# A decoder block in fp32 on one core: the opening's row tiles turned one by one, two channels to a bank, with fewer warming matmuls

## The chip, the core and the metric

One core of one Trainium2 chip runs the whole program. The metric is the device time of one execution in microseconds; lower is better. The kernel before took 797.24 us, the median of three runs (797.21 to 797.54). The profiles quoted below are of one further execution, in which the profiler ran along.

## The reference

Input is x, 512 positions of 1024 channels in fp32, and the parameters of one layer:

```
h = rmsnorm(x, norm1_g);  z = h @ w_in + b_in          # 1024 -> 6656 columns
z_glu, z_rx, z_rg, z_ga, z_gb = split(z)
u   = silu(layernorm(causal_conv31(z_glu[:1024] * sigmoid(z_glu[1024:]))))
y_a = u @ conv_w_out + conv_b_out
xb  = causal_conv4(z_rx);  hb = rg_lru(xb)              # gates from two block-diagonal products, a scan
y_b = (hb * gelu(z_rg)) @ lru_w_out
x   = x + (sigmoid(z_ga) * y_a + sigmoid(z_gb) * y_b) @ w_mix_out
h   = rmsnorm(x, norm2_g)
x   = x + (silu(h @ ffn_w1) * (h @ ffn_w3)) @ ffn_w2
out = rmsnorm(x, norm_f_g)
```

The change lies in the first line: the first normalization, the turn of its result so that channels lie on partitions, and the first two column blocks of the product with w_in.

## The kernel before, in words

**Precision and weights.** Every operand of a large product is split into a high part and a low part in the type fp32r, and a product is three matmuls: high weight by high input, high weight by low input, low weight by high input (`mm3`, line 525). Weights come in chunks of 128 columns (`w_in_chunk`, line 191; raw tile, high part, low part in `emit_chunk`, line 150, and `split_to`, line 121): SyncE issues the load of 512 KB, ScalarE casts the high part (line 123), GpSimd subtracts for the low part (line 119). `emit_to(n)` (line 180) emits chunks up to the n-th. In the opening the first two chunks' high parts are cast by VectorE, and the second one's low part also comes from VectorE: the class `Later` (line 145) only keeps the operands of that subtraction, and `norm1_rows` issues it at a place of its own (line 652).

**The opening.** x is loaded as four row tiles of 128 positions, each as two halves of 512 channels (`load_x`, line 488). For each row tile, `norm1_rows` (line 591) has ScalarE square and sum both halves (lines 550 and 556), VectorE and ScalarE make the inverse root (lines 551, 557, 558), and VectorE scale both halves in place (line 595). `turn_half` (line 567) then turns two row tiles: for each of the eight channel blocks c, TensorE turns a 128 x 128 block of either tile into a PSUM bank of its own (line 574), ScalarE writes the high part h1{c}h with norm1_g as scale (line 582) and VectorE the low part h1{c}l (line 583). norm1_g itself is loaded as a row block and turned by `rows_turned` (line 513; turn in line 517, copy to `par` in line 518); the other parameter rows follow in two more calls. "First half" below means row tiles 0 and 1 (positions 0 to 255), "second half" row tiles 2 and 3.

**The first products.** `early_mm(i, hf)` (line 602) multiplies column block 0 (i = 0) or 8 (i = 1) of w_in with one half of the positions, 256 columns wide, so that products can start when half of the input is turned; its matmuls stand under line 534. For the first half, the eight low-weight products stand last. All later products are 512 wide.

**Banks.** PSUM has eight banks of 128 x 512: six in the pool `bank`, two in `bank2`, given out in turn. A tile waits for the readers of the tile that had its bank before.

**Warming.** 21 matmuls of 128 x 128 on a tile of ones (line 506) stand ahead of everything on TensorE.

**Order.** The opening (lines 640 to 665) is under `manual_schedule`: TensorE, ScalarE, VectorE and SyncE keep the order in which the code stands there. GpSimd's order, and everything after, is set by the framework's scheduler. Waits are put in by the framework: an instruction waits for a count of the engine that it depends on, and dependences through PSUM are kept by the bank.

**After the opening** the kernel takes the other 50 column blocks of w_in, 24 matmuls each, with the convolutions, the gates and the scan beside them, then the products with lru_w_out, conv_w_out and w_mix_out, the feed-forward products (partly by a scheme with seven products instead of eight), and the last normalization. TensorE is given a product of some kind all the way.

Of the kernel before, what the change touches and what calls it, by code (L numbers as in the profile page):

```python
# [33 lines left out]
RAW = 4  # L34
HL = 5
AHEAD = 4
WARM = 21

FEW, MANY = 32, 112

# [46 lines left out]
def tile_block(ctx, tc, a, out):  # L87
# [19 lines left out]
    def bank(name):  # L107
        return psum.tile([P, T], F32, tag="mm", name=name)
# [404 lines left out]
    def rows_turned(c0, c1):  # L513
        pt = bank2(f"par_ps{c0}")
        for c in range(c0, c1, P):
            m = min(P, c1 - c)
            pe.transpose(pt[:, c - c0 : c - c0 + m], rowt[row_at(c)[0]][:m, :P], ident[:m, :m])
        vec.tensor_copy(par[:, c0:c1], pt[:, : c1 - c0])
        return pt

    def pc(name, i):
        return par[:, col[name] + i : col[name] + i + 1]


    def mm3(ps, ws, xs, lo_last=False):


        n = 3 * len(ws)
        i = 0
        three = [((wh, xh), (wh, xl), (wl, xh)) for (wh, wl), (xh, xl) in zip(ws, xs)]  # L530
        if lo_last:
            three = [q[:2] for q in three] + [q[2:] for q in three]
        for l, r in (q for qs in three for q in qs):
            pe.matmul(ps, l, r, start=i == 0, stop=i == n - 1)  # L534
            i += 1

    def w_tiles(key, kt, ahead=AHEAD):
        h, l = weights(key, ahead)
        return [(h[:, k, :], l[:, k, :]) for k in range(kt)]
# [21 lines left out]
    def rstd_of(halves, junk, between=None):  # L561
        begun = rstd_begin(halves[0], junk[0])
        if between:
            between()
        return rstd_end(begun, halves[1], junk[1])

    def turn_half(name, rows, gname, dest, hf, bk, some=range(ND), full=None):

        cs = slice(hf * 256, hf * 256 + 256)
        for c in some:  # L570
            ps = bk[c % len(bk)](f"{name}{hf}{c}")
            for t in range(2):
                src = rows[2 * hf + t][c // 4][:, (c % 4) * P : (c % 4 + 1) * P]
                pe.transpose(ps[:, t * P : (t + 1) * P], src, ident)  # L574
            g = pc(gname, c)
            h, l = (v[:, cs] for v in dest[c])
            if full:
                f = full[c][:, cs]
                newest["half"] = act.activation(f, ps[:, :256], AF.Copy, scale=g).ins
                _, _, last = split_to(h, l, f, vec)  # L580
                continue
            act.activation(h, ps[:, :256], AF.Copy, scale=g)
            last = vec.scalar_tensor_tensor(out=l, in0=ps[:, :256], scalar=g, in1=h.bitcast(F32), op0=ALU.mult, op1=ALU.subtract)
        return last.ins

    def parts_of(pair_tiles, cs=slice(0, T)):
        return [(h[:, cs], l[:, cs]) for h, l in pair_tiles]

    h1p = [pairt(f"h1{c}") for c in range(ND)]

    def norm1_rows(t, between=None):
        junk = [shortt(f"n1j{t}{h}") for h in range(2)]
        r = rstd_of(xt[t], junk, between)
        for h in range(2):
            vec.tensor_scalar(out=xt[t][h], in0=xt[t][h], scalar1=r, scalar2=None, op0=ALU.mult)

    HALVES = [slice(0, 256), slice(256, 512)]
    EARLY = 1
    EARLY_IN = [(GLU + j + 8 * o) for j in range(EARLY) for o in range(2)]
    early = []  # L600

    def early_mm(i, hf):
        m = EARLY_IN[i]
        if hf == 0:
            early.append((m, w_tiles(f"in{m}", ND, 0), bank(f"z{m}")))
        _, ws, ps = early[i]
        mm3(ps[:, HALVES[hf]], ws, parts_of(h1p, HALVES[hf]), lo_last=hf == 0)


    c4, c8 = (consts.tile([P, NR], F32, name=n) for n in ("c4", "c8"))  # L610
# [27 lines left out]

    ET = mybir.EngineType
    with tc.manual_schedule(engines={ET.PE, ET.Activation, ET.DVE, ET.SP}):  # L640
        norm1_rows(0)
        norm1_rows(1)
        rows_turned(0, ROWS[0][1])
        emit_to(1, vec.tensor_copy)
        turn_half("tx", xt, "norm1_g", h1p, 0, [bank, bank, bank, bank2])
        later = Later()
        emit_to(2, vec.tensor_copy, later)
        load_x(2)
        load_x(3)
        for i in first[1:]:  # L650
            load_rows(i)
        norm1_rows(2, lambda: vec.tensor_tensor(**later.operands))
        norm1_rows(3)
        for i in range(len(parts)):
            if i not in first:
                load_rows(i)
        early_mm(0, 0)
        early_mm(1, 0)
        turn_half("tx", xt, "norm1_g", h1p, 1, [bank2, bank, bank])
        emit_to(3)  # L660
        early_mm(0, 1)
        lru_factors(rows_turned(ROWS[0][1], n_first)[:, 2 * P :])
        emit_to(4)
        early_mm(1, 1)
        rows_turned(n_first, n_rows)
    h1 = parts_of(h1p)

# [623 lines left out]
```

## Time and profile before

| | |
|---|---|
| median of three runs | 797.24 us (797.21 to 797.54) |
| the profiled execution | 797.7 us |
| its span, first to last instruction | 795.9 us |
| first matmul on TensorE | 1.09 us |
| first product of w_in (line 534) | 10.70 us |
| first 512-wide product | 25.52 us |

Rows of the timeline have start and duration in us, engine, line, operation, what is written and read, the count of merged instructions, and in brackets the idle time before them with what ended it. PE is TensorE's matmuls, PEld its weight loads, DVE is VectorE, ACT ScalarE, POOL GpSimd, SPq the issue of DMAs by SyncE. Buffer numbers are left out, so `z<-h10h,hl_in` stands for each product with h10h. A turn shows as a matmul `tx<-ident,x`.

### The profile page before, as it was taken

The page shows a single profiled execution, that of the slowest core. Times are in us where ns is not written, and L with a number is a line of the kernel's source. Part 1 is how long each engine was busy: PE and PEld are TensorE (multiplying, and loading weights), DVE is VectorE, ACT ScalarE, POOL GpSimd, SP SyncE. Part 2 cuts the span into 40 slices and gives each one's busy share as a digit, 9 for nine tenths or more (in the row PEclk, how much of TensorE's full clock was granted, in tenths as well). Part 3 has the DMA queues.
Part 4 walks back from the last instruction along what each step waited for, and adds up shares of the span by engine and source line. Part 5 has one row for each costly group of instructions (what it writes and reads, how often), then busy time and mean ns, then how long its engine had stood idle before and what let it go on. Part 6 is the DMA issues. An engine that isn't in the chain of part 4 may idle for free.

```text
span 795.9 us, 12177 instructions
## 1 busy us (share of the span) xinstructions
PE 789.2 (99%) x4369; PEld 690.5 (87%) x4369; DVE 673.2 (85%) x1020; ACT 471.7 (59%) x683; POOL 228.8 (29%) x181
## 2 busy tenths in 40 slices
PE   9999999999999999999999999999999999999997
PEld 8888888888888888888888898999999999888885
DVE  6699899999989988786787889978878887889757
ACT  6646585987768855563335575545455555577443
POOL 1855766797666856030000000000000000000000
PEclk9999999999999999999999999999999999999999
DMA  6945646487555664368847545566555553676652
GB/s 213 257 130 143 187 144 208 121 247 208 173 168 173 213 182 120 128 203 263 276 160 243 172 134 158 131 171 181 155 133 133 133 133 106 210 258 207 198 173 106
DMA packets 184604, 140.29 MB, mean 176 GB/s; under 512 B 14259, under 2 KB 162143, under 8 KB 184543
## 3 DMA queue, kind: packets, MB, share of 16 engines
q1 hardware_dynamic: 183103, 134.27, 55.2%
q0 software_dynamic: 1440, 5.24, 3.5%
q8 instruction: 34, 0.56, 0.3%
q14 instruction: 27, 0.22, 0.1%
HBM read 113.79 MB, written 18.64 MB: 166 GB/s over the span
## 4 chain that ended last, share of the span: by engine, by line
PE 99%; DVE 0%; issue 0%; ACT 0%
PE z L534 36%; PE or L953 13%; PE ft L1080 7%; PE yb L534 7%; PE fa L1080 7%; PE fr L1080 6%; PE ya L534 5%; PE mxr L953 5%; PE fe L1080 4%; PE g L827 3%; PE fb L1080 2%; PE f L534 2%; PE warm L506 1%; PE f L1106 1%; PE tx L574 1%; PE th L574 0%
## 5 line engine op out<-in xcount | busy, mean ns | idle before, releaser
L702 DVE SCALAR_TENSOR_TENSOR cv<-u,par,cv 128x511 f32<-128x511 f32 (+19 forms) x240 | 162.4, 730 | 5.0 <-ACT cv L699 4.7
L119 POOL TENSOR_TENSOR hl_in<-raw_in,hl_in 128x1024 fp32r<-128x1024 f32 x51 | 123.5, 2426 | 83.1 <-ACT hl_in L123 69.6
L355 POOL DMA_DIRECT2D raw_fb<-raw_fb x10 | 8.7, 874 | 298.4 <-DVE raw_fb L357 186.1
L119 POOL TENSOR_TENSOR ows<-ows 128x256 f32<-128x256 f32 x66 | 56.7, 861 | 37.7 <-DMA ows<-in_ffn_w_dram 34.7
L123 ACT CAST hl_ft<-raw_fb 128x1024 fp32r<-128x1024 f32 x40 | 41.8, 1048 | 32.5 <-DVE raw_fb L357 17.0
L123 ACT CAST hl_in<-raw_in 128x1024 fp32r<-128x1024 f32 x50 | 52.1, 1043 | 10.4 <-PE z L534 6.6
L119 DVE TENSOR_TENSOR hl_ft<-raw_fb,hl_ft 128x1024 fp32r<-128x1024 f32 x40 | 48.5, 1220 | 7.0 <-ACT hl_ft L123 6.9
L119 DVE TENSOR_TENSOR hl_fb<-raw_fb,hl_fb 128x1024 fp32r<-128x1024 f32 x30 | 36.6, 1221 | 9.5 <-ACT hl_fb L123 9.3
L357 DVE TENSOR_TENSOR raw_fb<-raw_fb,raw_fb 128x1024 f32<-128x1024 f32 x20 | 24.5, 1225 | 20.3 <-DMA raw_fb<-in_ffn_w_dram 20.0
L534 PE MATMUL z<-h10h,hl_in 128*128 128x512 f32 (+1 forms) x108 | 41.5, 385 | 0.0
L534 PE MATMUL z<-h17h,hl_in 128*128 128x512 f32 (+1 forms) x108 | 41.1, 381 | 0.0
L534 PE MATMUL z<-h13h,hl_in 128*128 128x512 f32 (+1 forms) x108 | 41.1, 381 | 0.0
L534 PE MATMUL z<-h15h,hl_in 128*128 128x512 f32 (+1 forms) x108 | 41.1, 381 | 0.0
L534 PE MATMUL z<-h14h,hl_in 128*128 128x512 f32 (+1 forms) x108 | 41.1, 381 | 0.0
L534 PE MATMUL z<-h16h,hl_in 128*128 128x512 f32 (+1 forms) x108 | 41.1, 381 | 0.0
L534 PE MATMUL z<-h12h,hl_in 128*128 128x512 f32 (+1 forms) x108 | 41.1, 381 | 0.0
L534 PE MATMUL z<-h11h,hl_in 128*128 128x512 f32 (+1 forms) x108 | 41.1, 381 | 0.0
L123 ACT CAST hl_fb<-raw_fb 128x1024 fp32r<-128x1024 f32 x30 | 31.4, 1047 | 8.9 <-PE mxr L953 3.7
L119 DVE TENSOR_TENSOR hl_ob<-raw_ob,hl_ob 128x1024 fp32r<-128x1024 f32 (+1 forms) x23 | 27.0, 1174 | 11.0 <-ACT hl_ob L123 10.9
L123 ACT CAST hl_ob<-raw_ob 128x1024 fp32r<-128x1024 f32 (+1 forms) x23 | 23.3, 1015 | 21.6 <-PE or L953 10.8
L1080 PE MATMUL fe<-hs_0h,hl_ft 128*128 128x256 f32 x160 | 30.7, 283 | 0.0
L1080 PE MATMUL ft<-hs_1h,hl_ft 128*128 128x256 f32 x160 | 30.4, 283 | 0.0
(1016 smaller groups left out, 2610.0 us busy)
## 6 DMA issues: line engine op xcount, KB each, us to landing
raw_in<-in_w_in_dram SPq DMA_DIRECT2D x52, 512.0 KB
raw_fb<-in_ffn_w_dram SPq DMA_DIRECT2D x96, 256.0 KB
ows<-in_ffn_w_dram SPq DMA_DIRECT2D x44, 256.0 KB
os<-ows SPq DMA_DIRECT2D x22, 512.0 KB
raw_ob<-in_ffn_w_dram SPq DMA_DIRECT2D x33, 256.0 KB
raw_ot<-os SPq DMA_DIRECT2D x33, 256.0 KB
raw_lo<-in_lru_w_out_dram SPq DMA_DIRECT2D x16, 320.0 KB
raw_fb<-raw_fb POOLq DMA_DIRECT2D x10, 512.0 KB, 4.6
```

Source lines behind the costliest of these rows:

```text
L119: return eng.tensor_tensor(out=o, in0=x, in1=y, op=ALU.subtract)
L123: copy(h, full)
L355: pool_e.dma_start(out=q, in_=y, accum_op=ALU.add)
L357: vec.tensor_tensor(out=q, in0=q, in1=y, op=ALU.add)
L506: pe.matmul(wp[:, :P], ones, ones, start=True, stop=True)
L534: pe.matmul(ps, l, r, start=i == 0, stop=i == n - 1)
L574: pe.transpose(ps[:, t * P : (t + 1) * P], src, ident)
L702: vec.scalar_tensor_tensor(out=acc[c][:, s:], in0=u[c][:, : T - s], scalar=dw(c, s), in1=acc[c][:, s:], op0=ALU.mult, op1=ALU.add)
L827: pe.matmul(ps, l, r, start=k == 0, stop=k == len(mms) - 1)
L953: pe.matmul(banks[i], l_[:, ts], r_, start=start and n == 0, stop=stop and n == 2, skip_group_check=again)
L1080: pe.matmul(ps[:, HALVES[i]], lw[:, 4 * i + c, :], rx_, start=not (again or i or c or m), stop=bool(i and c == 3 and m == 2), skip_group_c ...
L1106: pe.matmul(plain_1[:, cs], l, r, start=k == 0 and m == 0, stop=k == ND - 1 and m == 2)
```

## The change

- The opening has 12 warming matmuls instead of 21.
- `turn_half` isn't used in the opening any more (it stays for the second normalization). `turn_rows` turns one row tile, all eight channel blocks, as soon as that tile is scaled; `split_rows` then makes the high and low parts of a half. Four banks take the eight channel blocks of a half: blocks c and c + 4 share a bank.
- The turn of norm1_g stands between the turns of row tiles 0 and 1 instead of ahead of both.
- In column block 0's product with the first half, three of the eight low-weight products (of channel blocks 0, 1 and 2) stand among the products that wait for the input: after block 5's, after block 6's, and again after block 6's.
- Row tiles 2 and 3 are normalized by `norm1_pair`: row tile 3's first sum of squares and its small VectorE instruction stand before the scaling of row tile 2.
- In the second half, the turns take two banks of `bank2` and two of `bank`.
- Some calls change places without a change in any engine's own order (`emit_to(3)` and `emit_to(4)` against `early_mm`).

```
-WARM = 21
+WARM = 12
...
-    def norm1_rows(t, between=None):
-        junk = [shortt(f"n1j{t}{h}") for h in range(2)]
-        r = rstd_of(xt[t], junk, between)
+    def scale_rows(t, r):
         for h in range(2):
             vec.tensor_scalar(out=xt[t][h], in0=xt[t][h], scalar1=r, scalar2=None, op0=ALU.mult)
 
+    def norm1_rows(t):
+        scale_rows(t, rstd_of(xt[t], row_junk(t)))
+
+    def norm1_pair(t, t2, later):
+        jk, jk2 = row_junk(t), row_junk(t2)
+        begun = rstd_begin(xt[t][0], jk[0])
+        vec.tensor_tensor(**later.operands)
+        r = rstd_end(begun, xt[t][1], jk[1])
+        begun = rstd_begin(xt[t2][0], jk2[0])
+        scale_rows(t, r)
+        scale_rows(t2, rstd_end(begun, xt[t2][1], jk2[1]))
...
+    def turn_rows(pairs, t):
+        for c in range(ND):
+            at_ = (c // 4) * 256 + (t % 2) * P
+            pe.transpose(pairs[c % 4][:, at_ : at_ + P], xt[t][c // 4][:, (c % 4) * P : (c % 4 + 1) * P], ident)
+
+    def split_rows(pairs, hf):
+        for c in range(ND):
+            ps = pairs[c % 4][:, HALVES[c // 4]]
+            g = pc("norm1_g", c)
+            h, l = (v[:, HALVES[hf]] for v in h1p[c])
+            act.activation(h, ps, AF.Copy, scale=g)
+            vec.scalar_tensor_tensor(out=l, in0=ps, scalar=g, in1=h.bitcast(F32), op0=ALU.mult, op1=ALU.subtract)
+
+    def early_mm(hf, order):
+        if not early:
+            early.extend((m, w_tiles(f"in{m}", ND, 0), bank(f"z{m}")) for m in EARLY_IN)
+        if order in (0, 1):
+            order = [(order, k, m) for k in range(ND) for m in range(3)]
+        left = [3 * ND] * len(early)
+        for i, k, part in order:
+            _, ws, ps = early[i]
+            (wh, wl), (xh, xl) = ws[k], (v[:, HALVES[hf]] for v in h1p[k])
+            l, r = ((wh, xh), (wh, xl), (wl, xh))[part]
+            left[i] -= 1
+            pe.matmul(ps[:, HALVES[hf]], l, r, start=left[i] == 3 * ND - 1, stop=not left[i])
...
     with tc.manual_schedule(engines={ET.PE, ET.Activation, ET.DVE, ET.SP}):
+        first_ps = [bank(f"tx0{i}") for i in range(ND // 2)]
+        later = Later()
         norm1_rows(0)
+        turn_rows(first_ps, 0)
         norm1_rows(1)
         rows_turned(0, ROWS[0][1])
+        turn_rows(first_ps, 1)
         emit_to(1, vec.tensor_copy)
-        turn_half("tx", xt, "norm1_g", h1p, 0, [bank, bank, bank, bank2])
-        later = Later()
+        split_rows(first_ps, 0)
         emit_to(2, vec.tensor_copy, later)
         load_x(2)
         load_x(3)
         for i in first[1:]:
             load_rows(i)
-        norm1_rows(2, lambda: vec.tensor_tensor(**later.operands))
-        norm1_rows(3)
+        norm1_pair(2, 3, later)
...
-        early_mm(0, 0)
+        order = [(0, k, m) for k in range(ND) for m in range(2)]
+        for at_, k in ((12, 0), (15, 1), (16, 2)):
+            order.insert(at_, (0, k, 2))
+        order += [(0, k, 2) for k in range(3, ND)] + [(1, k, m) for ms in ((0, 1), (2,)) for k in range(ND) for m in ms]
+        early_mm(0, order)
+        next_ps = [b(f"tx1{i}") for i, b in enumerate((bank2, bank2, bank, bank))]
+        turn_rows(next_ps, 2)
+        turn_rows(next_ps, 3)
+        split_rows(next_ps, 1)
+        emit_to(3)
         early_mm(1, 0)
-        turn_half("tx", xt, "norm1_g", h1p, 1, [bank2, bank, bank])
-        emit_to(3)
-        early_mm(0, 1)
         lru_factors(rows_turned(ROWS[0][1], n_first)[:, 2 * P :])
+        early_mm(1, 1)
         emit_to(4)
-        early_mm(1, 1)
         rows_turned(n_first, n_rows)
```

More of the change, by code (lines that the diff above doesn't have):

```diff
@@ L589, in tile_block, with row_junk @@
     h1p = [pairt(f"h1{c}") for c in range(ND)]
-    def norm1_rows(t, between=None):
-        junk = [shortt(f"n1j{t}{h}") for h in range(2)]
-        r = rstd_of(xt[t], junk, between)
+    def row_junk(t):
+        return [shortt(f"n1j{t}{h}") for h in range(2)]
+    def scale_rows(t, r):
         for h in range(2):
             vec.tensor_scalar(out=xt[t][h], in0=xt[t][h], scalar1=r, scalar2=None, op0=ALU.mult)
+    def norm1_rows(t):
[8 more added lines that the diff above has]
+        scale_rows(t2, rstd_end(begun, xt[t2][1], jk2[1]))
@@ L597, in tile_block @@
     HALVES = [slice(0, 256), slice(256, 512)]
-    EARLY = 1
-    EARLY_IN = [(GLU + j + 8 * o) for j in range(EARLY) for o in range(2)]
+    EARLY_IN = (GLU, GLU + 8)
     early = []
[L602 to L607, printed above, removed]
+    def turn_rows(pairs, t):
+        for c in range(ND):
+            at_ = (c // 4) * 256 + (t % 2) * P
+            pe.transpose(pairs[c % 4][:, at_ : at_ + P], xt[t][c // 4][:, (c % 4) * P : (c % 4 + 1) * P], ident)
```

## The prediction

> **What bounds the kernel now.** I read the page's first part and the chain first, then TensorE's waits, then the opening in order of time.
>
> ```profile
> span 795.9 us, 12177 instructions
> PE 789.2 (99%) x4369; PEld 690.5 (87%) x4369; DVE 673.2 (85%) x1020; ACT 471.7 (59%) x683; POOL 228.8 (29%) x181
> PE 99%; DVE 0%; issue 0%; ACT 0%
> ```
> ```profile
> PE warm L506 <- DVE ones L499: 1.1, 1, 1.1
> ```
>
> The second fence is the whole answer of TensorE's waits in the first 200 us; the later stretches, asked the same way, list none. After its first matmul TensorE never stands idle in this trace, and the chain that ends last is TensorE from 1.09 us on. So one microsecond that TensorE gains or loses in the opening is one at the end, unless a later producer comes too late. The program lists of the two kernels, with line and buffer numbers left out, are the same but for 9 warming matmuls, the order of some 60 TensorE instructions and one VectorE instruction. SyncE's and GpSimd's lists are identical, with every DMA issue, and so is ScalarE's; some of its waits differ. All that matters lies before 26 us.
>
> The opening of the kernel before, first half (start, duration, engine, line):
>
> ```profile
> 1.09 7.80 PE L506 MATMUL warm<-ones 128*128 128x128 f32 x42 [1.09 <-DVE ones L499]
> 2.60 0.38 SPq L483 DMA_DIRECT2D rows<-in_norm_g_dram  x1
> 5.69 0.89 DVE L595 TENSOR_SCALAR x<-x,stats 128x512 f32<-128x512 f32 x2
> 6.54 0.63 ACT L556 ACTIVATE n1j<-x 128x512 f32<-128x512 f32 x1
> 7.83 0.88 DVE L595 TENSOR_SCALAR x<-x,stats 128x512 f32<-128x512 f32 x2
> 8.82 0.22 PE L517 MATMUL par_ps<-ident,rows 8*128 8x8 f32 x1
> 8.97 1.97 PE L574 MATMUL tx<-ident,x 128*128 128x128 f32 x16
> 9.08 0.17 DVE L518 COPY par<-par_ps 128x8 f32<-128x8 f32 x1 [0.37 <-PE par_ps L517]
> 9.16 0.68 DVE L123 CAST hl_in<-raw_in 128x1024 fp32r<-128x1024 f32 x1
> 9.45 0.47 ACT L582 ACTIVATE h10h<-tx,par 128x256 fp32r<-128x256 f32 x1 [1.85 <-PE tx L574]
> 9.82 0.47 ACT L582 ACTIVATE h11h<-tx,par 128x256 fp32r<-128x256 f32 x1
> 9.93 2.40 POOL L119 TENSOR_TENSOR hl_in<-raw_in,hl_in 128x1024 fp32r<-128x1024 f32 x1 [8.62 <-DVE hl_in L123]
> 9.96 0.48 DVE L583 SCALAR_TENSOR_TENSOR h10l<-tx,par,h10h 128x256 fp32r<-128x256 f32 x1
> 12.71 0.47 DVE L583 SCALAR_TENSOR_TENSOR h17l<-tx,par,h17h 128x256 fp32r<-128x256 f32 x1
> 13.10 0.68 DVE L123 CAST hl_in<-raw_in 128x1024 fp32r<-128x1024 f32 x1
> 13.24 0.39 PE L534 MATMUL z<-h17l,hl_in 128*128 128x256 f32 x1
> ```
>
> Each warming matmul leaves two records. The low parts h10l to h17l leave VectorE every 0.393 us ((12.71 - 9.96) / 7), and TensorE's products follow each by 0.06 us (h17l ends at 13.18, its product starts at 13.24): they are paced by VectorE. Second half:
>
> ```profile
> 17.28 2.30 PE L574 MATMUL tx<-ident,x 128*128 128x128 f32 x16
> 17.70 0.47 ACT L582 ACTIVATE h10h<-tx,par 128x256 fp32r<-128x256 f32 x1 [1.22 <-PE tx L574]
> 18.21 0.48 DVE L583 SCALAR_TENSOR_TENSOR h10l<-tx,par,h10h 128x256 fp32r<-128x256 f32 x1 [0.61 <-ACT h10h L582]
> 18.75 0.20 PEld L574 LDWEIGHTS tx<-ident,x 128*128 128x128 f32 x2 [0.23 <-DVE h10l L583]
> 19.33 0.36 PE L534 MATMUL z<-h10h,hl_in 128*128 128x256 f32 x1
> 22.16 0.28 PE L534 MATMUL z<-h17h,hl_in 128*128 128x256 f32 x1
> 22.28 0.23 PE L517 MATMUL par_ps<-ident,rows 82*128 82x82 f32 x1
> ```
>
> Here the products run at 0.12 us each ((22.28 - 19.33) / 24) and aren't paced. The turns waited for banks (0.23 us at 18.75).
>
> **The change part by part.** Twelve warmers are 24 records, and this row is the first 24:
>
> ```profile
> 1.09 5.49 PE L506 MATMUL warm<-ones 128*128 128x128 f32 x24 [1.09 <-DVE ones L499]
> ```
>
> It ends at 6.58, the last record being 0.42 long on a step of 0.21, so the next instruction can go at 6.37. The 9 warmers taken out are worth nothing by themselves: in the kernel before the last one gave way at about 8.8, when the second row tile's scaling (7.83 + 0.88 = 8.71) had just ended. What replaces them is useful work: the first row tile is scaled by 6.58, and its 8 turns go from 6.37 to 8.07 at the slow step of 0.21. The turn of norm1_g follows by 8.2. Its 4 KB are issued at 2.60, right behind the second row tile, whose last half ScalarE takes at 6.54, so I take them as landed; the other bound is 8.82, where TensorE turns them here, and then the second tile's turns would begin at 8.97 and the fifth would be 0.6 later than below. All of this lies beside the scaling of the second tile.
>
> Second tile: its first half is scaled at 7.83 + 0.44 = 8.27, or 8.31 with the instruction's own 0.48; turns go at 8.37 with a step of 0.11 (16 in 1.97, the last 0.27 long). Now the bank sharing counts. Channels c and c + 4 lie in one bank, and in the changed program h10h's activation waits for TensorE's count 26: 12 warmers, 8 turns, norm1_g, and the **fifth** turn of the second tile, the one of channel 4. That starts at 8.81. In the kernel before h10h started 0.31 after the start of the second turn in the second half (17.28 + 0.11, h10h at 17.70) and up to 0.37 in the first (8.97 + 0.11, 9.45). With 0.31 it now starts at 9.12 and h10l 0.51 later, at 9.63. VectorE's copy of par and cast of the weights, no longer held up 0.37 us by par_ps, end at 9.47 and don't hold it. Gain 0.33 us. h14h to h17h now wait for h10l to h13l; h14h would go at 9.12 + 4 x 0.37 = 10.60 (the step from h10h to h11h), h10l ends at 10.11: free.
>
> Low-weight products: h17l ends at 9.63 + 7 x 0.393 + 0.475 = 12.86. Three of the eight low products stand before h17l's: the first after h15l's product, at about 12.24, and GpSimd's low weights are there at 9.47 + 0.09 + 2.40 = 11.96, a cover of 0.28; without it TensorE would stall by what is lacking. h16l's product is at 12.52, h17l's at 13.00. Then 29 products are left, where 8 + 24 were: 13.00 + 30 x 0.12 = **16.60 instead of 17.28**, 0.68 earlier. The second weights' cast ends at 13.45 and is needed at 13.72, a cover of 0.27.
>
> Fourth tile's statistics moved up: its VectorE instruction goes before the scaling of the third tile. By the rows
>
> ```profile
> 15.95 0.14 DVE L551 TENSOR_SCALAR stats<-stats 128x1 f32<-128x1 f32 x1
> 16.52 0.17 DVE L558 RECIPROCAL stats<-stats 128x1 f32<-128x1 f32 x1 [0.42 <-ACT stats L557]
> 16.72 0.88 DVE L595 TENSOR_SCALAR x<-x,stats 128x512 f32<-128x512 f32 x2
> ```
>
> it saves the 0.42 us of waiting; with the 0.33 from above the fourth tile is scaled at about 16.95 instead of 17.60, and the third by 15.9. Needed are the third at 16.60 and the fourth at 17.47. Nothing on the path; without it TensorE would wait up to 0.2 us.
>
> Second half. The third tile's 8 turns take 16.60 to 17.47, the fourth tile's fifth turn starts at 17.47 + 4 x 0.11 = 17.91, and h10h at 18.22, **0.52 later than the 17.70 of before**: before, two turns were enough for the first channel; now thirteen are. The bank waits are gone and the turns end at 18.35, but now the products are paced: h10l at 18.73, h17l at 18.73 + 2.75 = 21.48, ended at 21.95, its product at 22.01, the last one over at 22.25. Before: 22.28. The 0.68 us are given back but for **0.03 us**.
>
> What hangs behind the later h10h: ScalarE's next cast and GpSimd's subtraction.
>
> ```profile
> 21.74 2.39 POOL L119 TENSOR_TENSOR hl_in<-raw_in,hl_in 128x1024 fp32r<-128x1024 f32 x1 [9.41 <-ACT hl_in L123]
> ```
> ```profile
> 26.06 0.40 PE L534 MATMUL z<-h10h,hl_in 128*128 128x512 f32 x1
> ```
>
> The low weights come at 24.13 + 0.52 = 24.65 and are first used at 26.06: 1.4 us of cover, and later chunks' is larger. I take nothing from here on. Sum: -0.03 us on the profiled execution (797.7 us, of which 795.9 are span), whose own time stands 0.46 above the median of 797.24. Forecast **797.2 us**; 0.3 to either side for the latencies of 0.06 and 0.31 that I carried over.
>
> **The rivals.** A measurement of this kernel tells about 0.2%, 1.6 us, from no change.
>
> *Slower: the clock.* TensorE starts slow:
>
> ```profile
> 6.00:7.00 1.00, 1.00 (x6) 1.00 1.11 333
> 7.00:8.00 1.00, 1.00 (x11) 1.00 1.15 324
> ```
>
> Six warming records touch the microsecond before 7.0, eleven the one after (the clock column doesn't show the early rate, the count does): the rate doubles near 7.1, 6.0 us after the first matmul. With 12 warmers the matmuls end at 6.37, before that. If turns count as work, the release comes as before and my sum holds. If not, turns take 0.21 each, the second tile's end at 10.07, h10h starts at about 9.67, and every product takes about 0.23 instead of 0.12 (the ratio of the steps 0.21 and 0.11) until a release at R. TensorE is through the 48 products of the first half at R + 48 x 0.12 - (R - 10.07) x 0.12 / 0.23, not before 17.15 (h10h 0.55 late), and the second half takes 22.25 - 16.60 = 5.65 from there. A release without delay gives +0.55 us (797.8); one after another 6.0 us, R = 16.1, gives 18.7, so 24.4 at the mark of 22.28, +2.1 us (799.3). It is slower by over 1.6 us from R = 15.1 on. For it: the records above; against it: in the trace TensorE was never asked for turns while slow.
>
> The Trainium skill, TensorE: Matmul & The Clock Gate, section Part 4: PE-mode transpose, speaks for it: transposes do not count as busy in the same way for the clock gate. Its Part 1 has a free-running window of 3.4 us, which would put R near 13.9, an estimate from that page, and the time near 798.3; no run here shows it yet.
>
> *Faster: the shared bank costs less.* If h10h in the second half follows its own channel's turn at 17.47, it starts at 17.78, the last product is over at 21.81, and the time is 796.8; with the first half's h10h earlier too, 796.6. Against it stands the count of 26.
>
> The Trainium skill, PSUM — Partial Sum Buffer, section PSUM bank collisions raise a hardware error, says that two engines on one bank at once are an error, so a wait for the whole bank is to be expected; no run here shows a collision.
>
> *The change doesn't do what it says.* The covers of 0.28 and 0.27 are thin, and norm1_g may land late. If one of them is short, TensorE stalls ahead of the inserted low products or the second weights and only the 0.33 of the first half arrives: 0.35 less, 797.55.
>
> **How the numbers follow.** Forecast, 796.9 to 797.4: 0.52. Low products held up, 797.4 to 797.7: 0.12. Clock, 797.8 to 799.3: 0.24, of it 0.07 above 798.8. Faster, 796.5 to 796.9: 0.12. Range 796.6 to 798.2: all of the first two, most of the faster case, about half of the clock's. Faster by over 0.2%: 0.01, no case reaches 795.6. Slower by over 0.2%: 0.07. Within: 0.92.
>
> **What would show it.** Right: first h10h near 9.1, first product near 9.65, h17l's first product near 13.0, turns of the third tile near 16.6, second h10h near 18.2, norm rows' second turn (L517, 82 wide) near 22.25, and no wait of TensorE after it. Clock rival: turns with a step of 0.21 after 8.4, and products of 0.23. Faster rival: second h10h before 18.0. Low products: a TensorE wait on GpSimd near 12.2. A different time with all of these right would mean that something after 26 us moved.

## The result, and the profile after

The change made the kernel slower, by 0.2%: **799.19 us** (median of 13 runs, 797.69 to 801.25) beside 797.62 (13 runs, 797.21 to 798.79) for the kernel before, ratio 1.0021 (95% interval 1.0011 to 1.0030). The forecast was 797.2, its range ended at 798.2. The runs of the kernel before lie within 1.6 us, those of the changed kernel over 3.6.

The profiled execution after is the quickest of its 13 (797.69 us). From its page, the span, the busy times, and the chain by engine:

```profile
span 795.9 us, 12142 instructions
...
PE 787.4 (99%) x4351; PEld 687.9 (86%) x4351; DVE 673.9 (85%) x1020; ACT 471.7 (59%) x683; POOL 229.5 (29%) x181
...
PE 98%; DMA 0%; ACT 0%; DVE 0%; issue 0%; SPq 0%
```

18 matmul records and as many weight loads are gone, 36 TensorE instructions. Its opening, in order of time:

```profile
1.09 4.63 PE L506 MATMUL warm<-ones 128*128 128x128 f32 x24 [1.09 <-DVE ones L499]
...
5.32 0.88 DVE L596 TENSOR_SCALAR x<-x,stats 128x512 f32<-128x512 f32 x2
...
5.95 1.06 PE L619 MATMUL tx<-ident,x 128*128 128x128 f32 x8 [0.23 <-DVE x L596]
...
8.04 1.09 PE L619 MATMUL tx<-ident,x 128*128 128x128 f32 x8 [0.87 <-DVE x L596]
...
8.50 0.69 DVE L123 CAST hl_in<-raw_in 128x1024 fp32r<-128x1024 f32 x1
...
8.84 0.47 ACT L627 ACTIVATE h10h<-tx,par 128x256 fp32r<-128x256 f32 x1 [1.58 <-PE tx L619]
...
9.37 0.39 PE L642 MATMUL z<-h10h,hl_in 128*128 128x256 f32 x1 [0.24 <-ACT h10h L627]
...
12.81 0.28 PE L642 MATMUL z<-h17l,hl_in 128*128 128x256 f32 x1
...
16.41 1.91 PE L619 MATMUL tx<-ident,x 128*128 128x128 f32 x16
18.03 0.47 ACT L627 ACTIVATE h10h<-tx,par 128x256 fp32r<-128x256 f32 x1 [2.85 <-PE tx L619]
...
22.16 0.24 PE L517 MATMUL par_ps<-ident,rows 82*128 82x82 f32 x1
```

This is the forecast's course: the third tile's turns at 16.41 (forecast 16.60, before 17.28), the second h10h 1.62 us behind them, the 82-wide turn at 22.16 (22.25; before 22.28). All is 0.1 to 0.3 early because x was scaled at 5.32 and not at 5.69. So this execution can't show the loss. One that does is a second profile of the same kernel (experiment 1, an execution of 800.78 us), whose x came 0.58 later; the same points:

```profile
5.90 0.88 DVE L596 TENSOR_SCALAR x<-x,stats 128x512 f32<-128x512 f32 x2
...
8.53 1.09 PE L619 MATMUL tx<-ident,x 128*128 128x128 f32 x8 [0.78 <-DVE x L596]
...
9.86 0.38 PE L642 MATMUL z<-h10h,hl_in 128*128 128x256 f32 x1 [0.24 <-ACT h10h L627]
...
16.91 1.91 PE L619 MATMUL tx<-ident,x 128*128 128x128 f32 x16
18.53 0.47 ACT L627 ACTIVATE h10h<-tx,par 128x256 fp32r<-128x256 f32 x1 [2.85 <-PE tx L619]
...
22.66 0.23 PE L517 MATMUL par_ps<-ident,rows 82*128 82x82 f32 x1
```

The opening costs 0.38 us here (22.66 - 22.28). The last matmul ends 3.05 us later than in before (793.34 against 790.29), so **2.7 us are lost after the opening**. TensorE's waits from 30 us on, of this execution (fe and fr are PSUM tiles of feed-forward products, ft what ScalarE copies out of fr, and hl_ft holds the high and low parts of weights):

```profile
PE fe L1123 <- DVE hl_ft L119: 0.8, 1, 0.8
PE fr L1123 <- ACT ft L1223: 0.6, 1, 0.6
```

Before and the quick execution after have no such line. The first wait is near 513 us, in the feed-forward stage: the scheme's sum t1 of weights comes late. First the timeline of the kernel before, then of the second profile:

```profile
499.56 1.01 POOL L355 DMA_DIRECT2D raw_fb<-raw_fb  x1 [145.26 <-DVE raw_fb L357]
...
504.30 3.64 SPq L345 DMA_DIRECT2D raw_fb<-in_ffn_w_dram  x6
...
508.23 1.23 DVE L357 TENSOR_TENSOR raw_fb<-raw_fb,raw_fb 128x1024 f32<-128x1024 f32 x1 [0.73 <-DMA raw_fb<-in_ffn_w_dram]
...
510.57 1.23 DVE L119 TENSOR_TENSOR hl_ft<-raw_fb,hl_ft 128x1024 fp32r<-128x1024 f32 x1 [0.78 <-ACT hl_ft L123]
...
511.85 0.30 PEld L1080 LDWEIGHTS fe<-hs_0h,hl_ft 128*128 128x128 f32 x2
```
```profile
500.36 1.01 POOL L355 DMA_DIRECT2D raw_fb<-raw_fb  x1 [145.67 <-DVE raw_fb L357]
...
506.38 3.45 SPq L345 DMA_DIRECT2D raw_fb<-in_ffn_w_dram  x6
...
510.26 1.23 DVE L357 TENSOR_TENSOR raw_fb<-raw_fb,raw_fb 128x1024 f32<-128x1024 f32 x1 [1.95 <-DMA raw_fb<-in_ffn_w_dram]
...
512.60 1.22 DVE L119 TENSOR_TENSOR hl_ft<-raw_fb,hl_ft 128x1024 fp32r<-128x1024 f32 x1 [0.78 <-ACT hl_ft L123]
...
513.87 0.30 PEld L1123 LDWEIGHTS fe<-hs_0h,hl_ft 128*128 128x128 f32 x2 [0.96 <-DVE hl_ft L119]
```

This is the scheme of seven products for the pairs k = 1 to 4 of weight chunks, the "begun" pairs, whose first products stand ahead of it. GpSimd adds one weight quarter to another by a DMA that accumulates (line 355, sum t4). SyncE's next six loads need a buffer that this DMA reads and go 0.05 us after it has landed; VectorE's sum, ScalarE's cast and VectorE's low part follow, then TensorE. In either kernel TensorE loads the low part as a weight 0.05 us after it is made (510.57 + 1.23 = 511.80, loaded at 511.85; 513.82 and 513.87): the chain has **little slack**, though no wait is listed for before. In the second profile the DMA took 5.97 us instead of 4.69. Of these 1.28 us 1.0 stays lost at TensorE: matmul for matmul against before it is 0.80 us late ahead of this place, 1.95 at it and 1.80 behind it. The rest of the 2.7 us is lost at three more places, matched the same way: 0.4 near 472 us, ahead of any of these DMAs; 0.9 near 528, behind the second DMA (6.34 us instead of 4.57), whose late sum makes ScalarE's cast late and with it the copy of ft that TensorE waits for; and 0.4 near 541, behind the third.

How much a late landing costs can be read from the other traces. Measured against TensorE's own course, the first DMA lands 0.23 to 0.37 us later than in before in the quick execution after and in experiments 2 and 10, and nothing is lost at this place; 0.58 later costs 0.35 (5), and 0.9 to 1.3 later 0.9 to 1.0 (12, 11, 1). So there is a little slack here, up to about 0.4 us. Two of the three profiled executions of the changed kernel, after and 10, stay inside it and lose at most 0.14 us behind the opening. They are also the quickest of their 13 and 12, and that of experiment 1 is the second slowest of its 12: no profile shows a typical execution of the changed kernel.

Why that DMA is slower stands in the view of the DMA queues, cut to the time from its issue to its landing. In before, then in the second profile (q0 carries the accumulate DMA, q8 instructions):

```profile
q0 software_dynamic: 144, 0.52, 59.0%
issues: line engine op xcount, KB each, median us to landing
raw_fb<-raw_fb POOLq DMA_DIRECT2D x1, 512.0 KB, 4.7
```
```profile
q0 software_dynamic: 144, 0.52, 47.6%
q8 instruction: 1, 0.02, 1.3%
issues: line engine op xcount, KB each, median us to landing
raw_fb<-raw_fb POOLq DMA_DIRECT2D x1, 512.0 KB, 6.0
```

q8 fetches TensorE's own program, 34 blocks of some 16 KB over the span. In the feed-forward stage of before one comes about every 15.3 us, which at 0.12 us a matmul with its load is 128 of them, 256 instructions. With 36 instructions fewer ahead of it, a block's fetch comes later and falls into the accumulate DMA: counted from the first turn of the second normalization (near 454 us), the fetch near 500 us comes after 43.9 to 44.2 us in the eight traces with the old program length, after 45.0 with 20 instructions fewer (16) and after 45.8 to 46.5 in the ten with 36 fewer. In all traces of this study but the two with GpSimd's sums, 79 such DMAs with no q8 packet from 1.5 us before their issue to their landing took 4.48 to 4.57 us; 71 with one that began over 0.45 us after the issue took 4.49 to 6.34, in the middle 5.15; 18 with one in between 4.52 to 5.07.

The Trainium skill, Runtime: NRT & Kernel Launch, section Instruction fetch mechanics, has such blocks of 16 KiB and 256 instructions, fetched by the sequencer's own DMA queue, and calls the cost of crossing a boundary mostly hidden. The size agrees; the cost here isn't hidden, since it lies in another transfer.

### The profile page after: what moved, and what is told of

It reads as the page before. It is cut to its first block, busy times and chain, and to the rows that moved or that the text cites. A ratio compares the mean times of both kernels' runs of the same rounds, so it can differ in the third digit from the quotient of the medians.

```text
span 795.9 us, 12142 instructions
## 1 busy us (share of the span) xinstructions
PE 787.4 (99%) x4351; PEld 687.9 (86%) x4351; DVE 673.9 (85%) x1020; ACT 471.7 (59%) x683; POOL 229.5 (29%) x181
## 4 chain that ended last, share of the span: by engine, by line
PE 98%; DMA 0%; ACT 0%; DVE 0%; issue 0%; SPq 0%
PE z L534 34%; PE or L996 13%; PE ft L1123 7%; PE yb L534 7%; PE fa L1123 7%; PE fr L1123 6%; PE ya L534 5%; PE mxr L996 5%; PE fe L1123 4%; PE g L870 3%; PE fb L1123 2%; PE f L534 2%; PE z L642 2%; PE f L1149 1%; DMA x<-in_x_dram 0%; PE th L574 0%
## 5 line engine op out<-in xcount | busy, mean ns | idle before, releaser
L534 PE MATMUL z<-h10h,hl_in 128*128 128x512 f32 x100 | 39.1, 391 | 0.0
L534 PE MATMUL z<-h12h,hl_in 128*128 128x512 f32 x100 | 38.9, 389 | 0.0
L534 PE MATMUL z<-h11h,hl_in 128*128 128x512 f32 x100 | 38.9, 389 | 0.0
L534 PE MATMUL z<-h13h,hl_in 128*128 128x512 f32 x100 | 38.9, 389 | 0.0
L534 PE MATMUL z<-h14h,hl_in 128*128 128x512 f32 x100 | 38.9, 389 | 0.0
L534 PE MATMUL z<-h15h,hl_in 128*128 128x512 f32 x100 | 38.9, 389 | 0.0
L534 PE MATMUL z<-h16h,hl_in 128*128 128x512 f32 x100 | 38.9, 389 | 0.0
L534 PE MATMUL z<-h17h,hl_in 128*128 128x512 f32 x100 | 38.9, 389 | 0.0
```

## The experiments

Theory F, formed from experiments 1 to 4: the number of TensorE instructions ahead of 499 us sets where the fetches fall, and the accumulate DMAs carry that to TensorE. Rivals: the clock; the opening alone (O); the program's length by some other way (P). The shifts are against the trace of before: "opening" at the 82-wide turn (L517), "end" at the last matmul.

| run | TensorE instr. against before | first two accumulate DMAs, us | opening | end | median | before, beside it |
|---|---|---|---|---|---|---|
| before | 0 | 4.69, 4.57 | 0 | 0 | | |
| after | -36 | 4.95, 5.15 | -0.12 | +0.02 | 799.19 | 797.62 |
| 1, after again | -36 | 5.97, 6.34 | +0.38 | +3.05 | 799.90 | 797.89 |
| 2, before, 12 | -36 | 4.92, 5.14 | +1.57 | +1.68 | 800.05 | 797.89 |
| 3, after, 21 | 0 | 4.68, 5.07 | +0.83 | +1.44 | 798.98 | 797.89 |
| 5, before, 12 wide | -36 | 5.27, 5.16 | -0.38 | +0.65 | 798.65 | 797.56 |
| 6, after, 21 narrow | 0 | 4.69, 4.56 | +4.26 | +4.25 | 801.88 | 797.56 |
| 10, after, idle edit | -36 | 5.07, 5.14 | +0.10 | +0.11 | 799.46 | 797.69 |
| 16, before, 16 wide | -20 | 4.68, 5.27 | +0.35 | +0.72 | 798.40 | 797.69 |
| 17, after, 21 small | 0 | 4.68, 4.56 | +0.75 | +0.74 | 798.41 | 797.75 |
| 18, before, 27 small | +24 | 4.68, 4.56 | +0.18 | +0.09 | 797.76 | 797.75 |

**1. The changed kernel again**, no edit.

> The changed kernel once more, for a second trace and its spread. Theory C (clock: 12 warming matmuls can end before TensorE's half rate is released, and the turns don't bring the release): times spread again over some 3 us, from 797.7 to about 801, and whether the profiled execution is quick or slow is read from its first release: quick (797.7 to 798.2) with a release before 6.4 us, slow with warming records and turns at a step of 0.21 beyond 8.4 us and products at 0.23 instead of 0.12. Rival O (order: the bank waits and the new order cost the time): the spread is under 1 us around 799.2, products run at 0.12, and the loss shows as waits of TensorE after 26 us or in the second half.

Measured: 799.90 us (797.93 to 801.13), ratio 1.0022 (1.0013 to 1.0030). The loss is there again; its profile is the second one above. The full rate was there before the turns and every product takes 0.12 us, so the clock is not what made this execution slow. Theory C doesn't hold for it; TensorE's waits after 26 us are what O named.

**2 and 3. The number of warming matmuls exchanged**: before with 12, after with 21.

```
-WARM = 21        (2, in before)          -WARM = 12        (3, in after)
+WARM = 12                                +WARM = 21
```

> The kernel before with 12 warming matmuls instead of 21, nothing else. C: slower and wide, median 798.5 to 800, from about 797.3 to 801. O: as the kernel before, 797.6 with a spread of at most 1.6.

> The changed kernel with 21 warming matmuls, all of the new order kept. C: the spread falls to that of the kernel before (1.6 or less) and the median to 797.5 to 798.1 (the first tile's turns then wait for the warmers, which end at 7.5 to 9.0, so the first half gains 0 to 0.7 and the second half gives 0.5 back). O: stays at 799.2.

Measured: 2: 800.05, ratio 1.0030 (1.0019 to 1.0042); 3: 798.98, ratio 1.0013 (1.0005 to 1.0022). In 2 TensorE runs dry after the warming, and the clock falls back; its busy time by stretch (busy share and matmuls, granted clock, DMA):

```profile
7.00:8.00 1.00, 0.61 (x2) 0.72 1.11 335
9.00:10.00 1.00, 1.00 (x5) 0.50 1.05 333
...
15.00:16.00 1.00, 1.00 (x11) 1.00 0.15 44
```

That is the clock rival, seen in a kernel that waits 1.8 us for norm1_g, with 1.57 us lost in the opening; no profiled execution of the changed kernel shows a clock below 1.00 there (15, with the same first half, does). 3 loses more in the opening than after (+0.83) and is nevertheless 0.9 us quicker than 1 beside the same runs of before. So something other than the opening goes with the 21. The old program length doesn't remove all of it: 3 loses 0.6 us behind its opening, near 541 us, where its third DMA lands 0.9 us late.

**4. Turns in place of the warming matmuls**, in before.

```
-    for _ in range(WARM):
-        pe.matmul(wp[:, :P], ones, ones, start=True, stop=True)
+    for _ in range(2 * WARM):
+        pe.transpose(wp[:, :P], ones, ident)
```

> The kernel before with its 21 warming matmuls (42 records) replaced by 42 turns of the tile of ones, back to back from about 1.4 us on. If turns count as work for the clock: their step falls from 0.21 to 0.11 between 4.5 and 8 us and the time is 797.6 plus or minus 0.5. If they don't: all 42 run at 0.21, to about 10.2, the products after them start at half rate, and the time is 799 to 802.

Measured: 797.90, ratio 1.0001 (0.9992 to 1.0010). Turns release the clock:

```profile
4.00:5.00 1.00, 1.00 (x6) 1.00 0.86 226
5.00:6.00 1.00, 1.00 (x11) 1.00 1.02 329
```

The rate doubles near 5 us with nothing but turns issued. The rule that the prediction weighed (the Trainium skill, TensorE: Matmul & The Clock Gate, section Part 4: PE-mode transpose, that transposes don't count as busy in the same way) is not borne out here.

**5 and 6. Program length apart from the length of the warming.** In before, 12 wide warming matmuls; in after, 21 narrow ones.

```
-        pe.matmul(wp[:, :P], ones, ones, start=True, stop=True)
+        pe.matmul(wp[:, :224], ones, ones[:, :1].to_broadcast([P, 224]), start=True, stop=True)   # 5, WARM = 12
+        pe.matmul(wp[:, :72], ones, ones[:, :72], start=True, stop=True)                          # 6, WARM = 21
```

> The kernel before, but 12 warming matmuls of 224 columns in place of 21 of 128: the same TensorE time up to about 8.8 us ((24 x 224) / (42 x 128) = 1.0) with 36 TensorE instructions fewer (9 x 4). Theory F: TensorE's own program is fetched in blocks through the same DMA engines (q8), and where a block's fetch falls into a GpSimd accumulate DMA (L355) of the feed-forward stage that DMA takes 0.5 to 1.8 us longer, which TensorE then waits for. In the trace of before the fetches lie at 498.46, 513.76, 529.02 us, in that of after at 499.96, 518.19, 533.22. F expects the fetches here at the places of after (about 500, 518, 533), the L517 turn of the norm rows still near 22.3, and a median 0.5 to 2 us above that of before. Rival O (the opening alone sets the difference: what enters the first product later is lost at the end): nothing of the opening is changed, so the median of before within 0.3 us.

> The kernel after, but 21 warming matmuls of 72 columns in place of 12 of 128: the same TensorE time ((42 x 72) / (24 x 128) = 0.98) with as many TensorE instructions as before. Theory F expects the q8 fetches at the places of before (498.5, 513.8, 529.0) and a median only by the opening's 0.4 us above before, 798.2 to 798.5 beside a before of 797.9. Rival O expects the time of after: 1.6 to 2 us above before.

Measured: 5: 798.65, ratio 1.0014 (1.0005 to 1.0023): the opening of the profiled execution is 0.38 us **quicker** than that of before, and the kernel 1.1 us slower, against O. Of the 1.03 us that its trace loses behind the opening, 0.36 are lost near 472 us, the rest near 512 and 541. 6: 801.88, ratio 1.0051 (1.0039 to 1.0064). My edit 6 missed its aim: the narrow matmuls keep the step of 0.21, the last one starts at 9.9 us, and the clock is released only after 12 us. But all its 4.26 us are lost in the opening and none after it, as F says.

**7 and 8. The sums t4 by GpSimd itself**, in before and after.

```
-            pool_e.dma_start(out=q, in_=y, accum_op=ALU.add)
+            pool_e.tensor_tensor(out=q, in0=q, in1=y, op=ALU.add)
```

> The kernel before, with the ten sums t4 of the feed-forward weights made by GpSimd itself (a 128x1024 addition, about 2.4 us by the rows of its L119 operations) in place of an accumulate DMA of 4.5 to 6.3 us. Theory F and its more general form (the chain accumulate, six loads, VectorE sum, cast, low part has no slack to TensorE near 512, 526 and 541 us): 2 us of cover appears there, TensorE waits nowhere, and the median falls to the best time of before, 797.0 to 797.3, with a spread of under 0.6 us instead of 1.5 to 2. Rival O: no change of the median (797.9), since the opening is the same.

> The kernel after with the same exchange (ten sums by GpSimd itself). Theory F: the loss of the feed-forward stage goes, 0.3 to 0.5 us above the kernel of the same exchange on before, from the opening alone, near 797.5. Rival O: still 1.6 to 2 us above it.

Measured: 7: 798.85, ratio 1.0015 (1.0006 to 1.0024); 8: 799.49, ratio 1.0025 (1.0016 to 1.0034). The expected cover didn't come, for a reason of its own. Of 7:

```profile
499.06 2.73 POOL L355 TENSOR_TENSOR raw_fb<-raw_fb,raw_fb 128x1024 f32<-128x1024 f32 x1 [144.79 <-DVE raw_fb L357]
499.45 2.63 DVE L119 TENSOR_TENSOR hs<-hf,hf 128x256 f32<-128x256 f32 x1
```

VectorE's 128x256 subtraction took 2.63 us instead of 0.42 beside GpSimd's addition. That agrees with the Trainium skill, SBUF — State Buffer, section Who interferes with whom (a VectorE instruction with two inputs from SBUF contends with a GpSimd instruction that reads SBUF). The runs decide nothing on F, but the two kernels are 0.64 us apart with it, against 1.6 to 2 without.

**9 and 10. The turns of the two buffers for the quarters b12 and b22 exchanged** in every second begun pair, in before and after.

```
+                own = {}
+                if again and (BEGUN.index(k) % 2):
+                    for m in ("b22", "b12"):
+                        own[m] = wsums.tile([P, 1024], F32, tag="wsum", name=f"raw_f{m}_{k}")
...
-                    f_load(m, k)
+                    f_load(m, k, own.get(m))
```

> The kernel before, with the two buffers of the sums b12 and b22 taken in turns in the four begun pairs (every second pair takes b22's buffer first), so that the next pair's b12 goes to the buffer that the sum t2 has already left and no longer waits for the accumulate DMA. Theory F (fetch of TensorE's program slows the accumulate DMAs, whose landing the six loads, VectorE's sum, the cast and the low part hang on, without slack to TensorE): b12's loads go about 5 us earlier, TensorE waits nowhere near 512, 526 and 541, and the median is 0.2 to 0.7 us below that of before, near 797.2, with less spread. Rival O (the opening alone sets the difference): within 0.2 us of before.

> The kernel after with the same exchange of buffers. Theory F: the fetches still fall into the accumulate DMAs, which still take 4.9 to 6.3 us, but nobody waits for them; only the opening's 0.3 to 0.5 us is left above the same exchange on before, so 797.5 to 797.8. Rival O: 1.6 to 2 us above before, 799.2 or more.

Measured: 797.75, ratio 0.9996 (0.9987 to 1.0005), and 799.46 (797.77 to 804.60), ratio 1.0025 (1.0011 to 1.0040). The edit did nothing: every engine's instructions stayed in the order of the kernel it was made in. (Apparently a buffer goes to the tile that is first **written**, not first allocated; that was not tried apart.) These are two more measurements of the kernels before and after; the trace of 10 is the third of the changed kernel and loses only 0.01 us behind the opening.

**11 and 12. Own banks in the second half**, in after; 12 has the idle edit of 9 as well and is the same program.

```
-        turn_rows(next_ps, 2)
-        turn_rows(next_ps, 3)
-        split_rows(next_ps, 1)
+        turn_half("tx", xt, "norm1_g", h1p, 1, [bank2, bank2, bank, bank])
```

> The kernel after, but the second half of the opening turned channel by channel again, each channel in a bank of its own for its two turns (four banks in turns); the first half, the 12 warming matmuls, the low products and the statistics stay changed. The prediction's own step says the shared banks cost the second half 0.52 us at its first activation: expected is the second half's first activation 0.3 to 0.4 us after the third tile's first turn instead of 1.4 to 1.6, the 82-wide turn of the norm rows near 21.9 instead of 22.2 to 22.7, and by theory F (its fetches lie as in after) a median of 798.2 to 799.0, 0.4 to 0.9 below after. Rival O: 797.2, 0.4 below before.

> The kernel of own banks in the second half with the exchange of buffers as well. Theory F: both losses gone, the first half's gain of 0.3 to 0.4 us kept: 796.7 to 797.1, below before by 0.5 to 0.9 us and below the kernel before with the exchange alone by 0.3 to 0.4. Rival O: the same as the kernel of own banks without the exchange.

Measured: 799.22, ratio 1.0018 (1.0010 to 1.0027), and 799.07, ratio 1.0017 (1.0007 to 1.0027). The second h10h starts 0.42 us after the third tile's first turn (17.81 and 17.39 in 11) instead of 1.62, so the shared bank's price was right. The time hardly moves: the feed-forward stage takes 1.0 us in either trace (opening +0.54 and -0.19, end +1.55 and +0.82). F's forecast for 11, 798.2 to 799.0, is missed by 0.2.

**13, 14 and 15. The accumulate DMAs taken off the chain**: VectorE makes the sums t4 of the four begun pairs, in before, in after, and in 11.

```
-        elif n == "t4" or k in ADDING:
+        elif (n == "t4" and k not in BEGUN) or k in ADDING:
```

> The kernel before, with the sum t4 of the four begun pairs made by VectorE (1.22 us each by the rows of L357) in place of the accumulate DMA; the other six stay with GpSimd's DMA. Nothing in the chain to TensorE then hangs on an accumulate DMA before 556 us. Theory F (a fetch of TensorE's program inside an accumulate DMA makes it late): the next pair's loads go at about 502.6 instead of 504.3, VectorE's sum t1 about 0.5 us later than now since it has 1.22 us more to do; median 797.5 to 798.3. Rival P (the number of TensorE instructions acts through something else than these DMAs): no statement for this kernel by itself.

> The kernel after with the same exchange. Theory F: although the fetches of TensorE's program stay where they are in after, the excess is gone: within 0.5 us of the kernel before with the same exchange (the opening alone is left), about 1.2 us below after. Rival P: still 1.2 to 2 us above the kernel before with the same exchange.

> The kernel after with own banks in the second half and the sums t4 of the four begun pairs by VectorE. Theory F: 0.3 to 0.7 us below the kernel after with VectorE's sums, so at or below the kernel before with them, 797.2 to 798.0. Rival P: 1 to 1.5 us above the kernel before with VectorE's sums.

Measured: 798.33, ratio 1.0008 (0.9999 to 1.0017); 798.75, ratio 1.0014 (1.0005 to 1.0023); 798.59, ratio 1.0013 (1.0004 to 1.0022). VectorE's extra work costs before 0.6 us, at the upper edge of what was expected. **With it, after is 0.4 us above before instead of 1.6 to 2.0**, and its runs lie within 0.9 us instead of 3.2 to 6.8. Its fetches have not been moved, though the exchange also changes the order of some VectorE and ScalarE instructions of that stage, in both kernels. So most of the excess goes through these DMAs, and P is left with at most the 0.4. It isn't nothing: in the traces of 13 and 14 the opening differs by 0.05 us, and the rest of their difference arises near 472 us. 15 misses F's forecast (0.3 to 0.7 below 14): it is 0.16 below 14 and 0.26 above 13. One reservation: 13 to 18 ran on another chip than 1 and 10, and the unedited changed kernel wasn't timed beside them. The kernel before takes 797.6 to 797.9 on each of the chips.

**16. Half the shift**: before with `WARM = 16` and 168 columns, written as in 5.

> The kernel before, but 16 warming matmuls of 168 columns: the same TensorE time up to about 8.8 us, 20 TensorE instructions fewer (half of what 12 of 224 columns leave out). Theory F: the fetches come about 1 us later than in before (near 499.5, 515, 530), so the first falls at the start of its accumulate DMA and the second, which in before starts within 0.2 us of its own, falls well inside: a median between before and the 12 wide matmuls, 0.3 to 1 us above before. Rival O (the opening alone): before within 0.3 us.

Measured: 798.40, ratio 1.0010 (1.0001 to 1.0018), between before (797.69) and 5. The first DMA goes free (4.68), the second is hit (5.27).

**17 and 18. Small warming matmuls**: after with its old program length in the same time, and before shifted the other way.

```
-        pe.matmul(wp[:, :P], ones, ones, start=True, stop=True)
+        pe.matmul(wp[:64, :75], ones[:, :64], ones[:, :75], start=True, stop=True)   # 17, WARM = 21
+        pe.matmul(wp[:96, :97], ones[:, :96], ones[:, :97], start=True, stop=True)   # 18, WARM = 27
```

> The kernel after, but 21 warming matmuls of 64 weight columns by 75 instead of 12 of 128 by 128: 36 TensorE instructions more in about the same time (a step of 0.125 us each if the step is bound by the columns loaded and streamed; in the run with 72 columns streamed but 128 loaded it stayed at 0.213, so the load set it). What the run with narrow matmuls should have been: the opening of after with the program length of before. Theory F: the fetches lie outside the first two accumulate DMAs (which take 4.5 to 4.7 us), the excess of 1.2 to 1.5 us is gone: 797.7 to 798.3 beside a before of 797.7, if the clock's rate is released as in after; if the release comes later the opening tells by how much, and that is to be taken off. Rival P, that the change's own order of work costs it in the feed-forward stage: 799.2 or more.

> The kernel before, but 27 warming matmuls of 96 weight columns by 97 instead of 21 of 128 by 128: 24 TensorE instructions more in the same time (54 steps of 0.162 us are 8.7). Theory F: the fetches come about 1.4 us earlier than in before, ahead of all of the first four accumulate DMAs, which all take 4.5 to 4.7 us; TensorE waits for none of them and the median falls to the lower half of what before spreads over: 797.0 to 797.5, at or under before. Rival O: before within 0.2 us.

Measured: 17: 798.41, ratio 1.0009 (1.0000 to 1.0018): 0.66 us above before, where the changed kernel is 1.6 to 2.0 above (F's range ended at 798.3). Its warming is as short as that of after, and the lost time is that of the opening (+0.75, +0.74 at the end):

```profile
1.09 4.61 PE L506 MATMUL warm<-ones 128*64 128x75 f32 x42 [1.09 <-DVE ones L499]
```

18: 797.76, ratio 1.0001 (0.9992 to 1.0010): no change. F's forecast of 797.0 to 797.5 missed. The first two DMAs were free in before already, and their fetches come only 0.1 to 0.2 us earlier, not 1.4; the third and fourth DMA, of which 18 was to free both, still take 4.79 and 5.53 without TensorE waiting. No version that beats the kernel before came out of these runs.

## Why the prediction was wrong, point by point

- **"The program lists ... are the same ... All that matters lies before 26 us": wrong.** This step failed. A program that is the same from 26 us on, at another place in its blocks, is fetched at other times, and the fetch near 500 us then falls into the accumulate DMA (5.97 us instead of 4.69 in 1, 1.0 us of it lost at TensorE). Of the 1.6 to 2.0 us, what is left with the old program length is 0.66 (17), and without the accumulate DMAs 0.42 (14 against 13): 0.9 to 1.6 us come from it.
- **The slack behind it.** No wait in TensorE's list was taken as slack. The low part that ends at 511.80 and is loaded at 511.85 shows how little there was: by the landings above at most about 0.4 us.
- **The opening, first half: mechanism right, a term missing.** Every step came 0.1 to 0.3 us before its forecast in after, with an early x, and 0.2 to 0.4 us behind it in 1, with a late one. That the opening of the profiled execution after ends within 0.1 us of the forecast owes something to its early x. But the first product now comes at 9.4 instead of 10.7, ahead of what is sure to have landed. I gave covers for the low weights and the second weights; of the first weights I said that copy and cast "end at 9.47 and don't hold it", and not that their load must have landed by then. Of nine profiled executions with the changed first half and at most 12 matmuls' time of warming, five have VectorE wait 0.3 to 1.4 us for it and TensorE 0.5 to 1.6 (the most in 15):

```profile
9.80 0.69 DVE L123 CAST hl_in<-raw_in 128x1024 fp32r<-128x1024 f32 x1 [1.39 <-DMA raw_in<-in_w_in_dram]
...
10.64 0.36 PE L642 MATMUL z<-h10h,hl_in 128*128 128x256 f32 x1 [1.55 <-DVE hl_in L123]
```

  VectorE waits 0.3 to 1.1 us for the same load in five traces with the old first half (5, 9, 13, 16, 18), where TensorE then loses at most 0.8. How much of the median the opening took isn't separated: in the three profiled executions of the changed kernel its shift was -0.12, +0.38 and +0.10 us, where -0.03 was forecast, and the medians leave at most +0.4 (14 against 13) to +0.7 us (17 against before) for it and all else that isn't these DMAs.
- **The opening, second half: right.** The shared bank gives back the first half's gain: 1.62 us from turn to h10h, forecast 18.22 - 16.60 = 1.62.
- **Statistics moved up; the low products among paced ones: right**, no wait of TensorE shows there in the first two profiles of the changed kernel. (The fourth tile's 16.95 should be 16.85 by its own terms, 17.60 - 0.42 - 0.33; nothing hangs on it.)
- **Rivals.** Once it was released (at 4.7, 6.4 and 7.2 us) the clock stayed at the full rate in the three profiled executions of the changed kernel, and turns count (4). But the rival isn't dead: 2 shows what it costs when TensorE runs dry, and so does 15, which has the changed first half. There TensorE waits for the first weights, is busy for 0.09 and 0.36 us of the two microseconds from 9 to 11, and the granted clock is 0.50 from 11.4 to 14.8 us; its opening ends 1.5 us late. Slow executions of the changed kernel that weren't profiled may have lost time in this way. "The shared bank costs less" fell. "Low products held up" named the right kind of fault, a cover too thin, at the wrong load.
- **The last line of the prediction's tests** ("something after 26 us moved") names what happened, without giving it a rival or a price.

Open: how a fetch of 0.9 us makes an accumulate DMA up to 1.8 us longer, and one begun within 0.2 us of the issue hardly (4.56 and 4.57, once 5.07); and what the two slowest executions of 10 (803.46 and 804.60) lost, since they were not profiled. At 472 us four of the ten traces with 36 instructions fewer (1, 5, 8, 14), and none of the others, lose another 0.3 to 0.4 us; ScalarE waits there 1.8 to 1.9 us for a load of weights, 0.6 in before. That this is a fetch too was not tried.

## What to carry to other kernels

A change of the number of instructions shifts the fetches of the engine's program for all that follows; before calling the rest of a long kernel unchanged, look for chains through DMAs that end just when they are needed. No wait in the list of a bottleneck engine means no loss, not slack: compare the time a producer ends with the time its reader starts. Work pulled ahead of a first load needs that load's landing among its covers, over several executions and not one.

## What the runs showed of the hardware

- With one block of about 16 KB of TensorE's program, 0.9 to 1.7 us on the DMA engines, fetched inside it, a 512 KB accumulate DMA took up to 6.34 us, 5.15 in the middle of 71, instead of 4.5.
- Turns of 128x128 alone released TensorE's clock (the rate doubles near 5 us in 4).
- Warming matmuls of 72 columns with 128 weight columns kept the step of those with 128 columns (0.21 us), and the clock was released only after 12 us (6); with 64 weight columns and 75 columns (42 in 4.61 us) it came before 5 us (17). Each is one trace.
- A 128x256 VectorE subtraction beside a 128x1024 GpSimd addition took 2.63 us instead of 0.42 (7).
